# Two-layer hybrid diffusion block: ConvFFN down projections as seven block products, float32 activations kept on chip, six adaLN blocks moved earlier

## Chip, cores and metric

The kernel runs on one core of one Trainium2 chip. The metric is device time in microseconds of one execution; smaller is better. TensorE (PE in the rows) multiplies, VectorE (DVE) and ScalarE (ACT) prepare operands and empty the accumulator banks, and SyncE's queue (SP) issues every DMA of this kernel. PSUM has eight accumulator banks of 128x512 float32.

## What is computed

A latent stream of 1024 tokens and 1024 features passes two layers. Layer 0 mixes tokens by multi-scale pooling and windowed attention, layer 1 by a gated spatial MLP. Every layer ends with a ConvFFN, and every sublayer is normalized, modulated (adaLN: shift, scale, gate from a conditioning vector) and added to the stream:

```python
def post(x, y, g, gate):
    return x + gate * rmsnorm(y, g)

def conv_ffn(h, w_up, conv_w, conv_b, w_down):
    hu = h @ w_up                                   # 1024 -> 2*2816
    hcv = lax.conv_general_dilated(hu, conv_w[:, None, :], ...) + conv_b   # depthwise, width 3
    gate, up = jnp.split(hcv, 2, axis=-1)
    return (jax.nn.silu(gate) * up) @ w_down        # 2816 -> 1024: the down projection

    sh_m, sc_m, gt_m, sh_f, sc_f, gt_f = adaln(c, w_ada[i], b_ada[i])   # silu(c) @ w + b
    ...
    x = post(x, y, g_mix_post[i], gt_m)
    x = post(x, conv_ffn(pre(x, g_ffn_pre[i], sh_f, sc_f), ...), g_ffn_post[i], gt_f)
```

## The kernel before

**Precision.** Every large product takes its two float32 operands as a rounded part (float32r, "hi") and a remainder ("lo"). `three` (lines 123 to 127) issues three matmuls for each pair of tiles: hi by hi, hi by lo, lo by hi. Making the two parts of a 128x512 tile takes one copy on ScalarE and one subtraction on VectorE: `piece` (lines 113 to 121) does it for a weight tile that it loads into one of four `raw` buffers; its result goes into one of three `hl` buffers.

**Stages.** Layer 0: input projections (`u_proj`, `q_proj`), attention (16 units of `scores` and `attend`), output projection `e`, then `ffn`: the up projection with convolution and gating, which writes each of 22 gated feature blocks (128 features x 1024 tokens) to the DRAM tensor `act_d`, and the down projection `d`. Layer 1: projections `sv` and `su`, output projection `o`, `ffn` again. Instructions are written by hand in program order; a scheduler at build time turns this order into one fixed order for each engine and for SP's queue, and `tc.high_priority()` moves what stands under it ahead. Buffers are claimed when their former tile is done.

**Down projection before.** `load_acts(hf)` reads the 22 blocks of one token half (512 tokens), splits each into hi and lo and keeps them: eight blocks in the large rotating buffers `big` (six of 16 KB a partition), 14 in a pool of their own. `back_proj` then runs, for each output half `dh` and each of the 22 blocks, one `piece` of the weights and 12 matmuls into four banks (four blocks of 128 tokens). So one layer has 2 token halves x 2 output halves x 22 x 12 = 1056 matmuls. In layer 1 the second token half is done in two passes of two token blocks, so that each weight tile is split once more and serves six matmuls; the last of the post-processing then concerns two token blocks. Emptying a bank takes the sum of squares on ScalarE and a multiplication by the gate row `grows` on VectorE. `post_pair` (lines 272 to 306) normalizes two token blocks, adds the residual `xin` read from DRAM, stores the result, and, where a layer follows, normalizes again, transposes on TensorE and writes the modulated operand of the next stage.

**adaLN blocks.** `ada_sum(i)` reads a block of 1024x512 weights in four DMAs of 512 KB into the two `xtmp` buffers and does eight multiply-adds of 128x512 on VectorE into an `ntmp` buffer; `ada_finish(i)` sums over partitions on TensorE. Blocks 0 and 1 give a gate row and take two splits and two more DMAs. Blocks 0 and 1 stand at attention units 8 and 12, blocks 4, 5, 2, 3 behind the first half of the output projection `e`. The transposed probabilities `pt` of `attend` use the same two `xtmp` buffers.

Of the kernel before, what the change touches and what calls it, by code (L numbers as in the profile page):

```python
# [16 lines left out]
P = 128  # L17
# [24 lines left out]
def hybrid_block(ctx: ExitStack, tc: tile.TileContext, x, cx, cols_d, rows_d, cvw_d, rope_d, ident_d, mask_d, wada_a,  # L42
# [167 lines left out]
    def ada_sum(i):  # L210

        acc = ntmp(f"aacc{i}")[:, :HT]
        for q in range(4):
            raw = xtmp(f"ar{i}_{q}")
            nc.sync.dma_start(out=raw, in_=wada_b[i, q])
            for kk in range(2):
                k = 2 * q + kk
                w = raw[:, kk * HT:(kk + 1) * HT]
# [53 lines left out]
    def post_pair(y, hf, pair, ss, step, h, nxt, name, to_h=True):  # L272
# [23 lines left out]
        for kp in range(4):  # L296
            ps = bank(f"tr{name}{kp}")
            for kk in range(2):
                for i in range(2):
                    k = 2 * kp + kk  # L300
                    nc.tensor.transpose(out=ps[:, (2 * kk + i) * P:(2 * kk + i + 1) * P],
                                        in_=y[:, 2 * pair + i, k * P:(k + 1) * P], identity=ident)
            tsl = slice(2 * pair * P, 2 * (pair + 1) * P)
            modulated(ps, 2, 2 * P, 2 * kp, lambda k: gmod[:, l, w, k:k + 1],
                      lambda k: ada[:, l, 24 * w + k:24 * w + k + 1], h[0][:, 2 * kp:2 * kp + 2, tsl],
                      h[1][:, 2 * kp:2 * kp + 2, tsl], f"{name}{kp}", kp % 2 == 1)
# [13 lines left out]
    def post(ys, hf, step, nxt, name):  # L320
        h = hslots("h" + name) if nxt is not None else None
        for pair in range(2):
            post_pair(ys[0], hf, pair, ys[1], step, h, nxt, f"{name}{pair}")
# [45 lines left out]
    def ffn(l, pu, h0, tail, step, nxt, background=()):  # L369
# [163 lines left out]

        es = ExitStack()
        ap = es.enter_context(tc.tile_pool(name=f"act{l}", bufs=NF - 8, reuse_waits="tile"))
        act, acts_hh = {}, {}

        def new_act(f, hf):

            if f >= 8:  # L540
                return ap.tile([P, 2, HT], F32R, tag="a", name=f"a{l}_{f}_{hf}")
            s = f // 4
            if (s, hf) not in acts_hh:
                acts_hh[s, hf] = slot([P, 4, 2, HT], F32R, f"ah{l}_{s}_{hf}")
            return acts_hh[s, hf][:, f % 4]

        def load_acts(hf):
            for f in range(NF):
                raw = ntmp(f"arw{l}_{f}_{hf}")[:, :HT]
                nc.sync.dma_start(out=raw, in_=act_d[order[f]][:, halves(hf)])  # L550
                t = act[f] = new_act(f, hf)
                A.copy(out=t[:, 0, :], in_=raw)
                tt(t[:, 1, :], raw, t.bitcast(F32)[:, 0, :], ALU.subtract)

        def acts(f):
            return act[f][:, 0, :], act[f][:, 1, :]

        load_acts(0)
        ys = back_proj(pu, acts, lambda k: wdn[l, order[k]], NF, 0, step, f"d{l}")
        load_acts(1)  # L560
        h0 = post(ys, 0, step, nxt, f"f{l}0")
        if nxt is not None:
            ys = back_proj(pu, acts, lambda k: wdn[l, order[k]], NF, 1, step, f"d{l}")
            es.close()
            return h0, ys
        y = slot([P, 4, D], F32, f"yd{l}1")
        for pair in range(2):
            ys = back_proj(pu, acts, lambda k: wdn[l, order[k]], NF, 1, step, f"d{l}", (2 * pair, 2 * pair + 1), y)
            post_pair(y, 1, pair, ys[1], step, None, None, f"f{l}1{pair}")
# [3 lines left out]
    with ExitStack() as es:  # L573
# [123 lines left out]
        with tc.tile_pool(name="rope", bufs=1) as rp:  # L697
# [86 lines left out]
            for j in range(4):  # L784
                q_proj(j)

# [98 lines left out]
        order = [(n, kv) for n in range(8) for kv in range(2)]  # L885
        for i, (n, kv) in enumerate(order):
# [19 lines left out]
        for i in (4, 5, 2, 3):  # L906
            ada_block(i)
# [3 lines left out]
    h0, ys = ffn(0, pu, h0, lambda b22, ts: post_sums(ys, 0, (0, 1), "a1", h0, b22, ts), 1, (1, 0), range(6, 12))  # L911


    with ExitStack() as es:
        cs = es.enter_context(tc.tile_pool(name="cs", bufs=1))
# [41 lines left out]
        h.append(post(ys, 1, 1, (1, 0), "f01"))  # L957
# [5 lines left out]
        mp = es.enter_context(tc.tile_pool(name="mp", bufs=1))  # L963
# [129 lines left out]
```

## Time and profile before

| | us |
|---|---|
| three timed runs, median (lowest to highest) | 2151.49 (2147.37 to 2152.92) |
| the profiled execution, its own time | 2150.81 |
| its span, first to last instruction | 2149.0 |

The profile is of one execution, 1.8 us longer than its span. Busy time of an engine is the union of its instructions. Matmuls overlap in the pipeline, so that the rate is read from counts in a window and not from the duration of one.

### The profile page before, as it was taken

To read this page: it belongs to the slowest core of one execution; us is meant where nothing else is said; L and a number is where in the kernel's file an instruction comes from. 1 tells how busy PE (TensorE), PEld (TensorE's weight loads), DVE (VectorE), ACT (ScalarE), POOL (GpSimd) and SP (SyncE) were. 2 spreads that over 40 slices of the span, in tenths; PEclk is the share of its full clock that TensorE was granted. 3 is DMA by queue.
4 is the path that set the end of the run, shared out by engine and by line. 5 is a ranking of instruction groups with operands and counts; after the bars stand their busy time and mean duration, and the time that the engine had idled before them with its cause. 6 is when DMAs were issued, how large, how long until landed. Compare 5 with 4: busy or idle time off the path is not lost.

```text
span 2149.0 us, 26048 instructions
## 1 busy us (share of the span) xinstructions
PE 2083.5 (97%) x9334; PEld 1635.6 (76%) x9334; DVE 1523.3 (71%) x2403; ACT 1092.4 (51%) x1892; POOL 0.2 (0%) x4
## 2 busy tenths in 40 slices
PE   6999988999999999999999999999999999999998
PEld 2786545777877888888787888887878888888876
DVE  4687765668999987854634567467998897774655
ACT  5646754357555555544524432256655554553544
POOL 0000000000000000000000000000000000000000
PEclk8999999999999999999999999999999999999999
DMA  8110012747444442255524336346644222164675
GB/s 307 53 49 23 6 50 95 233 150 274 164 164 164 170 142 89 96 179 171 182 95 162 102 115 197 111 161 237 210 138 161 98 98 89 69 211 146 206 246 181
DMA packets 123985, 311.25 MB, mean 145 GB/s; under 512 B 13768, under 2 KB 14408, under 8 KB 123728
## 3 DMA queue, kind: packets, MB, share of 16 engines
q1 hardware_dynamic: 123856, 309.60, 43.1%
q8 instruction: 73, 1.20, 0.2%
q14 instruction: 56, 0.46, 0.1%
HBM read 260.26 MB, written 49.28 MB: 144 GB/s over the span
## 4 chain that ended last, share of the span: by engine, by line
PE 76%; DVE 10%; DMA 7%; ACT 4%; issue 2%; SPq 0%; DVEq 0%; ACTq 0%
PE d L126 6%; PE d L125 6%; PE d L127 6%; PE x L125 5%; PE x L127 4%; PE x L126 4%; PE o L869 3%; PE z L126 3%; PE z L125 3%; PE z L127 3%; DMA ar<-in_wada_b_dram 2%; DMA rawd<-in_wdn_dram 2%; PE xb L125 2%; PE xb L126 2%; PE xb L127 2%
## 5 line engine op out<-in xcount | busy, mean ns | idle before, releaser
L51 DVE TENSOR_TENSOR hld<-rawd,hld 128x512 fp32r<-128x512 f32 x220 | 150.8, 691 | 212.3 <-ACT hld L119 210.1
L119 ACT CAST hld<-rawd 128x512 fp32r<-128x512 f32 x220 | 136.7, 622 | 257.0 <-PE d L127 200.6
L398 ACT CAST w<-s 128x512 fp32r<-128x512 f32 x176 | 108.8, 620 | 226.1 <-PE z L127 107.5
L126 PE MATMUL d<-hld,a 128*128 128x512 f32 x448 | 175.1, 391 | 0.7 <-DVE hld L51 0.5
L125 PE MATMUL d<-hld,a 128*128 128x512 f32 x448 | 174.8, 390 | 0.2 <-ACT hld L119 0.2
L127 PE MATMUL d<-hld,a 128*128 128x512 f32 x448 | 174.4, 389 | 0.0
L51 DVE TENSOR_TENSOR w<-s,w 128x512 fp32r<-128x512 f32 x176 | 120.4, 686 | 32.9 <-ACT w L398 32.8
L48 DVE SCALAR_TENSOR_TENSOR aacc<-ar,silc,aacc 128x512 f32<-128x512 f32 x140 | 104.7, 748 | 20.7 <-DMA ar<-in_wada_b_dram 19.5
L48 DVE SCALAR_TENSOR_TENSOR au<-c,cvw,au 128x1023 f32<-128x1023 f32 x88 | 112.6, 1280 | 1.0
L126 PE MATMUL d<-hld,ah 128*128 128x512 f32 x256 | 100.2, 392 | 0.4 <-DVE hld L51 0.3
L127 PE MATMUL d<-hld,ah 128*128 128x512 f32 x256 | 99.7, 389 | 0.0
L125 PE MATMUL d<-hld,ah 128*128 128x512 f32 x256 | 99.6, 391 | 0.0
L126 PEld LDWEIGHTS d<-hld,a 128*128 128x128 f32 x448 | 84.1, 188 | 20.2 <-DVE hld L51 3.0
L125 PEld LDWEIGHTS d<-hld,a 128*128 128x128 f32 x448 | 84.1, 188 | 18.5 <-ACT hld L119 1.1
L127 PEld LDWEIGHTS d<-hld,a 128*128 128x128 f32 x448 | 84.1, 188 | 17.3
L869 PE MATMUL o<-pt,vv 128*64 128x512 f32 x152 | 78.7, 637 | 7.6 <-ACT pt L867 7.4
L125 PE MATMUL x<-t,w 128*128 128x512 f32 x208 | 82.0, 394 | 0.9 <-ACT c L477 0.9
L51 DVE TENSOR_TENSOR s<-raw 128x512 f32<-128x512 f32 x88 | 60.6, 689 | 29.7 <-DMA raw<-in_wup_dram 28.6
L126 PE MATMUL x<-t,w 128*128 128x512 f32 x208 | 81.4, 391 | 0.0
L127 PE MATMUL x<-t,w 128*128 128x512 f32 x208 | 81.3, 391 | 0.0
L127 PE MATMUL z<-b,w 128*128 128x512 f32 x176 | 69.3, 394 | 0.0
L126 PE MATMUL z<-b,w 128*128 128x512 f32 x176 | 69.3, 394 | 0.0
(458 smaller groups left out, 5596.5 us busy)
## 6 DMA issues: line engine op xcount, KB each, us to landing
rawd<-in_wdn_dram SPq DMA_DIRECT2D x220, 256.0 KB, 2.9
raw<-in_wup_dram SPq DMA_DIRECT2D x88, 512.0 KB, 4.5
ar<-in_wada_b_dram SPq DMA_DIRECT2D x80, 512.0 KB, 4.3
actd<-ag SPq DMA_DIRECT2D x44, 512.0 KB, 2.9
arw<-actd SPq DMA_DIRECT2D x88, 256.0 KB, 3.6
ra<-in_wup_dram SPq DMA_DIRECT2D x36, 256.0 KB, 3.4
leadd<-c SPq DMA_DIRECT2D x18, 512.0 KB, 4.2
aw<-in_wada_a_dram SPq DMA_DIRECT2D x16, 512.0 KB, 6.9
```

What stands on the lines that cost most here:

```text
L48: V.scalar_tensor_tensor(out=out, in0=in0, scalar=scalar, in1=in1, op0=op0, op1=op1)
L51: V.tensor_tensor(out=out, in0=in0, in1=in1, op=op)
L119: A.copy(out=hi, in_=raw)
L125: nc.tensor.matmul(ps, a[0], b[0], start=first, stop=False, skip_group_check=more)
L126: nc.tensor.matmul(ps, a[0], b[1], start=False, stop=False, skip_group_check=more)
L127: nc.tensor.matmul(ps, a[1], b[0], start=False, stop=last, skip_group_check=more)
L398: A.copy(out=t[:, 0, :], in_=src)
L869: nc.tensor.matmul(po, vv[:, kb, a], pt, start=c == 0, stop=c == nch - 1)
```

## The change

Both token halves are now in one product scheme. With the 22 feature blocks split in two halves j (11 each) and the output in two halves, each layer's down projection is a product of 2x2 blocks: A (token halves hf by feature halves j) times B (feature halves by output halves), done by seven block products of 11 steps with 12 matmuls each. The products run in the order 5, 1, 3, 6, 2, 7, 4, on two sets of four banks, and several accumulate onto a bank set that has been copied out. Their operands are sums and differences of blocks, formed on VectorE in float32 at each step and split into hi and lo at each step; two sums of weight blocks are written to DRAM scratch (`t1d`, `t2d`) and read again three products later. The activations stay as float32 in the six `big` buffers. Results collect in two tiles `ys` of a new pool; the gate row is now applied in `post_pair` (`gated=False`), with one more VectorE addition of 128x1024 for each token block and the modulation wholly on ScalarE. The second half of layer 1 is no longer done in pairs. adaLN blocks 0 and 1 go behind `q_proj(1)` and `q_proj(3)`; blocks 4, 5, 2, 3 go to attention units 3, 6, 9, 12, finish two units later, and load 256 KB at a time into the `raw` buffers.

```diff
-    def ada_sum(i):
+    def ada_sum(i, short=False):
+            if short:
+                ws = [raw_tile(f"as{i}_{q}{kk}") for kk in range(2)]
+                for kk in range(2):
+                    nc.sync.dma_start(out=ws[kk], in_=wada_b[i, q][:, halves(kk)])
...
-            stt(yb, yb, r[:, i:i + 1], xin, ALU.mult, ALU.add)
+            if gated:
+                stt(yb, yb, r[:, i:i + 1], xin, ALU.mult, ALU.add)
+            else:
+                stt(yb, yb, r[:, i:i + 1], grows[step], ALU.mult, ALU.mult)
+                tt(yb, yb, xin, ALU.add)
...
-        load_acts(0)
-        ys = back_proj(pu, acts, lambda k: wdn[l, order[k]], NF, 0, step, f"d{l}")
-        load_acts(1)
-        h0 = post(ys, 0, step, nxt, f"f{l}0")
...
+        dp = dn.enter_context(tc.tile_pool(name=f"dn{l}", bufs=3, reuse_waits="tile"))
...
+        def act(hf, j, k, load=False):
+            i = 2 * k + j
+            if (hf, i // 8) not in acts:
+                acts[hf, i // 8] = slot([P, 8, HT], F32, f"ac{l}_{hf}_{i // 8}")
+            t = acts[hf, i // 8][:, i % 8, :]
+            if load:
+                nc.sync.dma_start(out=t, in_=act_d[order[j * nh + k]][:, halves(hf)])
+            return t
...
+        def operands(prod, k):
+            if prod == 5:
+                s_ = act(1, 0, k, True)
+                tt(s_, s_, act(1, 1, k, True), ALU.add)
+                t_ = summed("t1" + nm, wload(0, k, 1, "b12" + nm), wload(0, k, 0, "b11" + nm), ALU.subtract, t1d, k)
+            elif prod == 1:
+                s_ = act(0, 0, k, True)
+                tt(act(1, 0, k), act(1, 0, k), s_, ALU.subtract)
+                t_ = wload(0, k, 0, "b11" + nm)
+            elif prod == 3:
+                s_ = summed("s4" + nm, act(0, 1, k, True), act(1, 0, k), ALU.subtract)
+                t_ = wload(1, k, 1, "b22" + nm)
+            elif prod == 6:
+                s_ = act(1, 0, k)
+                t_ = summed("t2" + nm, wload(1, k, 1, "b22" + nm), scratch(t1d, k, "t1r" + nm), ALU.subtract, t2d, k)
+            elif prod == 2:
+                s_ = act(0, 1, k)
+                t_ = wload(1, k, 0, "b21" + nm)
+            elif prod == 7:
+                s_ = summed("s3" + nm, act(1, 1, k), act(1, 0, k), ALU.subtract)
+                t_ = summed("t3" + nm, wload(1, k, 1, "b22" + nm), wload(0, k, 1, "b12" + nm), ALU.subtract)
+            else:
+                s_ = act(1, 1, k)
+                t_ = summed("t4" + nm, wload(1, k, 0, "b21" + nm), scratch(t2d, k, "t2r" + nm), ALU.subtract)
+            for src, pool, tag in ((s_, dp, "sa"), (t_, wp, "hl")):
+                t = pool.tile([P, 2, HT], F32R, tag=tag, name=f"{tag}{nm}")
+                A.copy(out=t[:, 0, :], in_=src)
+                tt(t[:, 1, :], src, t.bitcast(F32)[:, 0, :], ALU.subtract)
...
+        def down_product(prod, banks, first):
+            for k in range(nh):
+                with tc.high_priority():
+                    sa, w = operands(prod, k)
+                for b in range(4):
+                    three(banks[b], tuple(sa[:, i, b * P:(b + 1) * P] for i in range(2)), (w[:, 0, :], w[:, 1, :]),
+                          first and k == 0, k == nh - 1, not first)
...
+        y = y_banks("p5")
+        down_product(5, y, True)
+        evac(y, 1, 1, False, False)
+        x_ = [pu(f"px{l}{b}") for b in range(4)]
+        down_product(1, x_, True)
+        evac(x_, 0, 0, False, False)
+        down_product(3, y, False)
+        evac(y, 0, 1, False, False)
+        down_product(6, x_, False)
+        evac(x_, 0, 1, True, True)
+        y = y_banks("p2")
+        down_product(2, y, True)
+        evac(y, 0, 0, True, True)
+        h0 = post((ys[0], ss[0]), 0, step, nxt, f"f{l}0", False)
+        down_product(7, x_, False)
+        evac(x_, 1, 1, True, True)
+        down_product(4, x_, False)
+        evac(x_, 1, 0, False, True)
...
             for j in range(4):
                 q_proj(j)
+                if j in (1, 3):
+                    ada_block(j // 2)
...
+        late = {3: 4, 6: 5, 9: 2, 12: 3}
...
-            if i in (8, 12):
-                acc = ada_sum(i // 4 - 2)
-            if i in (9, 13):
-                ada_finish(i // 4 - 2, acc)
+            if i in late:
+                acc = ada_sum(late[i], True)
+            if i - 2 in late:
+                ada_finish(late[i - 2], acc)
...
-        for i in (4, 5, 2, 3):
-            ada_block(i)
```

## Rows read from the trace of the kernel before

**Rows 1.** The page: span, busy time by engine, the chain that ended last by engine.
```profile
span 2149.0 us, 26048 instructions
...
PE 2083.5 (97%) x9334; PEld 1635.6 (76%) x9334; DVE 1523.3 (71%) x2403; ACT 1092.4 (51%) x1892; POOL 0.2 (0%) x4
...
PE 76%; DVE 10%; DMA 7%; ACT 4%; issue 2%; SPq 0%; DVEq 0%; ACTq 0%
```

**Rows 2.** Windows: stretch, length; busy us (instructions) by engine, granted clock, DMA share, GB/s.
```profile
500.00:880.00 380.00, 376.67 (x1652) 304.11 (x1651) 344.09 (x469) 207.62 (x312) 0.00 (x0) 1.00 0.45 154
915.00:1161.00 246.00, 245.27 (x1093) 201.43 (x1092) 115.19 (x183) 100.59 (x187) 0.00 (x0) 1.00 0.46 149
1896.00:2140.00 244.00, 242.73 (x1057) 197.21 (x1056) 133.23 (x203) 112.99 (x202) 0.00 (x0) 1.00 0.63 200
...
1100.00:1150.00 50.00, 50.00 (x222) 41.19 (x221) 14.51 (x22) 12.66 (x25) 0.00 (x0) 1.00 0.31 97
```

**Rows 3.** The same view: stages of the adaLN blocks, in order q projections, attention, `e`.
```profile
110.00:160.00 50.00, 50.00 (x230) 41.36 (x228) 41.56 (x76) 23.76 (x41) 0.00 (x0) 1.00 0.16 50
...
270.00:290.00 20.00, 14.08 (x70) 7.71 (x69) 14.26 (x29) 9.33 (x21) 0.00 (x0) 0.91 0.37 129
...
320.00:350.00 30.00, 24.35 (x112) 13.56 (x112) 20.22 (x45) 15.09 (x33) 0.00 (x0) 0.83 0.27 88
380.00:400.00 20.00, 17.21 (x69) 13.66 (x69) 14.11 (x22) 6.16 (x14) 0.00 (x0) 0.91 0.67 223
```

**Rows 4.** Groups of instructions by form: line, engine, operation, count, busy us, mean ns.
```profile
L51 DVE TENSOR_TENSOR hld<-rawd,hld 128x512 fp32r<-128x512 f32 x220 | 150.8, 691 | 212.3 <-ACT hld L119 210.1 <-DMA arw<-actd 2.0
L119 ACT CAST hld<-rawd 128x512 fp32r<-128x512 f32 x220 | 136.7, 622 | 257.0 <-PE d L127 200.6 <-DMA rawd<-in_wdn_dram 24.3 <-DVE hld L51 19.7
...
L48 DVE SCALAR_TENSOR_TENSOR aacc<-ar,silc,aacc 128x512 f32<-128x512 f32 x140 | 104.7, 748 | 20.7 <-DMA ar<-in_wada_b_dram 19.5
```

**Rows 5.** Timeline of DVE near the end of layer 0's up projection: start, duration.
```profile
896.92 0.68 DVE L51 TENSOR_TENSOR ah<-arw,ah 128x512 fp32r<-128x512 f32 x1
897.51 0.68 DVE L51 TENSOR_TENSOR w<-s,w 128x512 fp32r<-128x512 f32 x1
898.12 1.28 DVE L51 TENSOR_TENSOR ah<-arw,ah 128x512 fp32r<-128x512 f32 x2
...
918.06 2.60 DVE L48 SCALAR_TENSOR_TENSOR au<-c,cvw,au 128x1023 f32<-128x1023 f32 x2
```

**Rows 6.** Windows of high and middling DMA load (columns as in rows 2).
```profile
10.00:20.00 10.00, 9.33 (x20) 1.76 (x18) 0.00 (x0) 3.31 (x6) 0.00 (x0) 1.00 1.02 414
...
2030.00:2070.00 40.00, 39.29 (x166) 30.42 (x165) 22.56 (x33) 18.14 (x33) 0.00 (x0) 1.00 0.81 270
2110.00:2140.00 30.00, 30.00 (x134) 24.86 (x133) 15.62 (x23) 13.82 (x25) 0.00 (x0) 1.00 0.53 158
```

**Rows 7.** DMA issues of 2030 to 2070: count, size, median us to landing.
```profile
rawd<-in_wdn_dram SPq DMA_DIRECT2D x29, 256.0 KB, 4.0
xinf<-x3d SPq DMA_DIRECT2D x4, 512.0 KB, 4.7
```

**Rows 8.** DMA issues of 2110 to 2140 (columns as in rows 7).
```profile
rawd<-in_wdn_dram SPq DMA_DIRECT2D x17, 256.0 KB, 3.0
```

**Rows 9.** Timeline of PE: end of the last first-stage product; bank change in `e`.
```profile
896.04 0.39 PE L125 MATMUL z<-b,w 128*128 128x512 f32 x1
...
392.06 0.50 PE L125 MATMUL e<-hle,hix 128*128 128x512 f32 x1 [2.79 <-DVE ye L51]
...
394.96 0.63 PE L125 MATMUL e<-hle,hix 128*128 128x512 f32 x1
```

**Rows 10.** Timeline of the last 10 us: ACT, DVE, SP.
```profile
2139.80 0.60 ACT L163 ACTIVATE junk<-d 128x512 bf16<-128x512 f32 x1 [2.78 <-PE d L127]
...
2142.97 2.48 DVE L48 SCALAR_TENSOR_TENSOR yd<-yd,rpf,xinf 128x1024 f32<-128x1024 f32 x2
...
2144.29 1.54 SPq L284 DMA_DIRECT2D out_dram<-yd  x2
```

More of the change, by code (lines that the diff above doesn't have):

```diff
@@ L208, in ada_first @@
             ALU.mult)
-    def ada_sum(i):
+    def ada_sum(i, short=False):
         acc = ntmp(f"aacc{i}")[:, :HT]
         for q in range(4):
-            raw = xtmp(f"ar{i}_{q}")
-            nc.sync.dma_start(out=raw, in_=wada_b[i, q])
+            if short:
[3 more added lines that the diff above has]
+            else:
+                raw = xtmp(f"ar{i}_{q}")
+                nc.sync.dma_start(out=raw, in_=wada_b[i, q])
+                ws = [raw[:, halves(kk)] for kk in range(2)]
             for kk in range(2):
                 k = 2 * q + kk
-                w = raw[:, kk * HT:(kk + 1) * HT]
+                w = ws[kk]
                 if k == 0:
@@ L269, in modulated, with post_pair @@
         tt(lo, fv, hi.bitcast(F32), ALU.subtract)
-    def post_pair(y, hf, pair, ss, step, h, nxt, name, to_h=True):
+    def post_pair(y, hf, pair, ss, step, h, nxt, name, to_h=True, gated=True):
         s2 = sm.tile([P, 2], F32, tag="s2", name="s2" + name)
@@ L318, in back_proj, with post @@
         return y, ss
-    def post(ys, hf, step, nxt, name):
+    def post(ys, hf, step, nxt, name, gated=True):
         h = hslots("h" + name) if nxt is not None else None
         for pair in range(2):
-            post_pair(ys[0], hf, pair, ys[1], step, h, nxt, f"{name}{pair}")
+            post_pair(ys[0], hf, pair, ys[1], step, h, nxt, f"{name}{pair}", gated=gated)
         return h
@@ L532, in ffn @@
             assert not background
+        nh = NF // 2
         es = ExitStack()
[L535 to L556, printed above, removed]
-        load_acts(0)
-        ys = back_proj(pu, acts, lambda k: wdn[l, order[k]], NF, 0, step, f"d{l}")
@@ L560, in ffn @@
-        load_acts(1)
-        h0 = post(ys, 0, step, nxt, f"f{l}0")
-        if nxt is not None:
[L563 to L569, printed above, removed]
+        yp = es.enter_context(tc.tile_pool(name=f"y{l}", bufs=2, side="right", reuse_waits="tile"))
@@ new lines, in wload, with scratch, summed @@
+        def wload(j, k, half, name):
+            t = raw_tile(name)
+            nc.sync.dma_start(out=t, in_=wdn[l, order[j * nh + k]][:, halves(half)])
+            return t
+        def scratch(t, k, name):
+            r = raw_tile(name)
+            nc.sync.dma_start(out=r, in_=t[k])
+            return r
+        def summed(name, in0, in1, op, keep=None, k=0):
+            t = dp.tile([P, HT], F32, tag="sum", name=name, bufs=4)
+            tt(t, in0, in1, op)
+            if keep is not None:
+                nc.sync.dma_start(out=keep[k], in_=t)
+            return t
@@ new lines, in down_product, with y_at, evac @@
+        def down_product(prod, banks, first):
[5 more added lines that the diff above has]
+                          first and k == 0, k == nh - 1, not first)
+        def y_at(hf, b, dh):
+            return ys[hf][:, b, halves(dh)]
+        def evac(banks, hf, dh, add, done):
+            for b in range(4):
+                if add:
+                    tt(y_at(hf, b, dh), banks[b], y_at(hf, b, dh), ALU.add)
+                else:
+                    A.copy(out=y_at(hf, b, dh), in_=banks[b])
+                if done:
+                    square_sum(y_at(hf, b, dh), ss[hf][:, 2 * b + dh:2 * b + dh + 1], HT)
@@ new lines, in y_banks @@
+        def y_banks(name):
+            return [mbank(f"{name}{l}0")] + [bank(f"{name}{l}{b}") for b in range(1, 4)]
+        y = y_banks("p5")
[9 more added lines that the diff above has]
+        y = y_banks("p2")
@@ L570, in ffn @@
+        down_product(2, y, True)
[5 more added lines that the diff above has]
+        evac(x_, 1, 0, False, True)
+        dn.close()
+        if nxt is not None:
+            return h0, (ys[1], ss[1]), es
+        post((ys[1], ss[1]), 1, step, None, f"f{l}1", False)
         es.close()
@@ L955, in v_norm @@
                                 scalar2=rs[:, n:n + 1], op0=ALU.subtract, op1=ALU.mult)
-        h.append(post(ys, 1, 1, (1, 0), "f01"))
+        h.append(post(ys, 1, 1, (1, 0), "f01", False))
+        ye.close()
         vs.append(slot([P, 4, D], F32, "vs1"))
@@ L962, in hybrid_block @@
         v_norm(1)
[L963 removed]
+        mp = es.enter_context(tc.tile_pool(name="mp", bufs=1, reuse_waits="tile"))
         ms = []
```

17 lines of the change are left out of this document (14 added, 3 removed).

## Prediction

> **What bounds the kernel now.** I read the page first: TensorE is busy 97% of the span and holds 76% of the chain that ended last; VectorE has 71% [rows 1]. Then the windows, stage by stage, since a mean hides limits. In the up projection TensorE is full and VectorE is at 344.09 of 380 us; in both down projections TensorE is full, VectorE has only 115 of 246 and 133 of 244 us [rows 2]. So the stage that is changed is bound by the number of its matmuls, with room on the engines that prepare operands. The rate is 222 matmuls in 50 us, 0.2252 us each, 2.70 us for a step of twelve, at a granted clock of 1.00, the 2.4 GHz level [rows 2]. Layer 1's stage holds 1057 in 244.0 us, where that rate would need 238.0: 6.0 us go to its passes over pairs, at their worst 166 matmuls in 40 us instead of 178 [rows 6]. The adaLN blocks have their own stages: TensorE idles 5.9 of 20 and 5.7 of 30 us around the two in attention, at clocks 0.91 and 0.83, and 2.8 of 20 us in `e` [rows 3].
>
> **What is removed.** Seven products of 11 steps of 12 are 924 matmuls a layer, 132 fewer than 1056. Two layers: 264 x 0.2252 = 59.5 us. The pairs of layer 1 go as well: 6.0 us. Together **-65.5**, if the new operands arrive in time. Four steps decide that.
>
> **VectorE and ScalarE in a step.** Before, a step needed one weight split and, half the time, one activation split. Now it needs two splits (two VectorE operations, two ScalarE copies) and sums: in the order 5, 1, 3, 6, 2, 7, 4 VectorE has 4, 3, 3, 3, 2, 4, 3 operations. ScalarE's two copies take 2 x 0.622 = 1.24 us of 2.70 [rows 4]: covered. One VectorE operation lasts 0.691 us [rows 4], which would make products 5 and 7 cost 2.76 us a step, more than TensorE. But queued ones start 0.59 and 0.61 us apart [rows 5], so four take 2.44. The Trainium skill ("VectorE: DVE Perf Modes", The DRAIN you can't avoid) has the next operation start only when the pipe is empty; starts closer than the duration disagree with it as I read it. By its rule the 44 steps of products 5 and 7 would cost 0.06 us more each, 2.6 us; by the rows nothing. I take the rows. The cover is thin: 0.26 us a step.
>
> **Start of product 5.** Layer 0's convolution still runs when the stage begins: VectorE does multiply-adds of 2.60 us a pair from 918.06 [rows 5], in all some 6 us behind 915, and its result is the last activation that product 5 loads. Slack in product 5 is 11 x 0.26 = 2.9 us. So 3 us late, per layer. The new operand pool also lies over buffers of the up projection, which come free with its last product: another 1 to 2 us (estimate: one chain of sum, copy and remainder, 0.61 + 0.62 + 0.69).
>
> **DMA.** Product 5 moves per step two activation tiles, two weight tiles and one scratch write, 5 x 262,144 bytes; 14.4 MB in 29.7 us. At 2030 to 2070 a share of 0.81 moved 270 GB/s, so a full share is 333, and 14.4 MB take 43 us [rows 6]. But the buffers of the up projection's first operand come free at 896.04 [rows 9], 19 us before 915, so 16 activation tiles (4.2 MB) can come early, and the remaining 10.2 MB need 31 us. Between 1 and 13 us late; with small transfers I take 4, as the rows of early release are direct. The Trainium skill ("DMA: Bandwidth & Descriptors", Specifications) gives about 358 GB/s as a core's HBM limit, which speaks against this product: 14.4 MB would take 40 us. The slice 10 to 20 moved 414 GB/s [rows 6], above that limit, so I do not use it; at 414 it would be 35. Start and DMA of product 5 together: 9 us a layer, **+18**, bounds +2 (all hidden) and +36 (18 a layer).
>
> Products 6, 7 and 4 also use two raw tiles a step, four buffers in all: two steps (5.40 us) must hold issue, landing, queueing and subtraction. Landing was 3.0 us at 158 GB/s and 4.0 at 270 [rows 6 to 8]. Product 6 runs at 3 x 262,144 / 2.70 us = 291 GB/s. Before, the same depth in time (four tiles of 1.35 us) lost 7% at 270 GB/s and nothing at 158 [rows 6]. So product 6 loses 7 to 8% of 29.7, 2.5 us a layer: **+5** (0 to 16). Products 7 and 4 need 194 GB/s, plus the residuals that `post` moves: 5%, or 1.5 us each, and between them the same four banks are reused at once, with VectorE adding each out; `e` lost 2.79 us at such a change, and matmuls of half clock (0.63 instead of 0.39) behind it [rows 9]. I take 1 here, since down stages show little such loss: **+8** for both layers (0 to 20).
>
> **post.** The gate row and the residual take two operations of about 1.22 us instead of one of 1.24 [rows 10]. For layer 0's first half VectorE has 4 x 2.44 + 8 x 0.61 + about 4 of normalizing = 19 us. Products 7 and 4 take 77 x 0.61 = 47, their bank adds and those before them 5: 71 us against 59.5 of matmuls and some 4 of transposes. Three buffers let 7.3 us be done earlier. The stage behind needs this result: **+3** (0 to 10). In layer 1 nobody waits for the first half; its rest falls into the end.
>
> **The end.** Now the last matmul ends at 2139.80 and the span at 2149.0: 9.2 us, with two multiply-adds, 2.48 us [rows 10]. Afterwards four token blocks are open, 4 x 2.44 = 9.8 us: 7.3 more, with two residual buffers whose loads take 4.7 us [rows 7], partly hidden. **+7** (5 to 10).
>
> **adaLN blocks.** A block is 8 multiply-adds, about 7 x 0.75 + 0.5 = 5.7 us of VectorE [rows 4]. In attention the two present blocks cost 5.9 + 5.7 us idle and up to 1.8 + 5.1 us of clock, 18 in all [rows 3]; there loads take `xtmp` buffers that the probabilities need. The four new ones use raw buffers, no gate row and smaller loads, but come four times: I leave 2 us each, gain 10 (bounds 0 and 18). `e` loses its four blocks: idle 2.8 and slow clock 1.8, gain 5 (0 to 8). The q projections get two blocks with gate splits, 15 us of VectorE where 8.4 of 50 are free and TensorE has no gap [rows 3]; later projections take the rest: cost 4 (0 to 10). Their DMAs are eight of 512 KB on SP's queue at a share of 0.16, hidden. Net **-11**.
>
> **Sum.** -65.5 - 11 + 18 + 5 + 8 + 3 + 7 = -35.5. The profiled execution took 2150.8, 0.7 below the median; 2150.8 - 35.5 = **2115 us**.
>
> **Rivals.**
> *Everything is covered.* TensorE full at the start of product 5 and through 6, 7, 4; only the end costs. 2150.8 - 65.5 - 11 + 7 + 2 = 2083. For it: VectorE's 242 operations a layer are 148 of 208 us. Against: 49 MB a layer in 208 us are 236 GB/s, over 149 and 200 before [rows 2].
> *VectorE paces products 5 and 7 and the posts.* If the 0.26 us of slack is lost to waits for ScalarE (0.62) in one of two steps, 44 x 0.31 = 14 us come on top, and 10 with the convolution's tail and `post`: 2115 + 24 = 2139. The up projection runs with VectorE at 91% and little loss [rows 2], which speaks against it.
> *Slower: the raw buffers' round trip.* In the 88 steps of products 5, 6, 7, 4 the time of a step is half a round trip: landing plus about 2.0 us (two issues, a place in VectorE's queue, 0.69). At landing 3.0 it is 2.5, hidden; at 4.0 it is 3.0, 26 us lost, near the 31 of my sum; at 5.5 it is 3.75: 92 us lost, 61 above the sum, 2176. It decides from 4.9 us of landing on (3.45 a step, 66 lost). 4.0 at 270 GB/s [rows 7] is short of that, but residuals took 4.7.
> *The change does little:* gains and new waits cancel, within 6.5 us (0.3%, about what a measurement here can tell): 2145 to 2158.
>
> **Chances.** Forecast (2095 to 2132) 0.55; all covered (2070 to 2095) 0.17; VectorE (2132 to 2145) 0.14; cancels 0.04; slower 0.10. That is faster 0.86, same 0.04, slower 0.10. The range leaves out most of the slower case and the best end: 2080 to 2150; the forecast's own is 2095 to 2132.
>
> **What would show it.** 1848 matmuls in the two down stages, each stage 215 to 235 us. Product 5 should show fewer than 222 in 50 us, products 1, 3 and 2 full. Landing of weight tiles near 4 us in 5 and 6. From the last matmul to the end 15 to 18 us. In attention no slice with 4 us of idle. Wrong: product 2 not full (then it is no operand problem), landing above 5, or VectorE above 95% through the stage.

## Result and profile after

The changed kernel takes 2165.15 us (median of four runs, 2160.87 to 2166.09) beside 2151.88 (2147.37 to 2152.92) for the kernel before on the same chip: ratio 1.0062 [1.0042, 1.0082], slower by 13 us. The forecast was 2115, range 2080 to 2150: wrong in sign. Its profiled execution took 2160.87 us.

The page of the changed kernel, the same lines as in [rows 1]:

```profile
span 2159.1 us, 25709 instructions
...
PE 2024.0 (94%) x9070; PEld 1586.3 (73%) x9070; DVE 1628.1 (75%) x2571; ACT 1109.4 (51%) x1940; POOL 0.2 (0%) x4
...
PE 68%; DVE 14%; DMA 11%; ACT 4%; issue 2%; SPq 1%; DVEq 0%; ACTq 0%
```

264 matmuls are gone, TensorE's busy time fell by 59.5 us, and the span grew by 10.1: on the chain, VectorE and DMA now hold 25% where they held 17%. The windows say in which stages. Up projection, layer 0's down stage, a middle product of it, layer 1's down stage (columns as in [rows 2]):

```profile
500.00:880.00 380.00, 377.26 (x1649) 305.75 (x1649) 340.97 (x458) 202.52 (x300) 0.00 (x0) 1.00 0.41 141
896.00:1153.00 257.00, 220.96 (x955) 179.07 (x956) 182.51 (x292) 125.02 (x236) 0.00 (x0) 0.92 0.58 193
960.00:1010.00 50.00, 50.00 (x222) 41.43 (x221) 28.57 (x45) 22.51 (x40) 0.00 (x0) 1.00 0.32 101
1889.00:2140.00 251.00, 215.29 (x924) 175.65 (x924) 172.83 (x271) 108.39 (x201) 0.00 (x0) 0.93 0.57 191
```

The count of matmuls is as forecast (924 a layer, 222 in 50 us where operands are there), but TensorE idles 36 us in each down stage. From the timelines, layer 0's down stage begins at 895.8 (915.4 before), lasts 257.5 us (245.2 before), layer 1's 251.1 (244.1), and the last matmul ends 19.4 us before the span does (8.7). So: 19.6 us won ahead of the first down stage, 12.3 and 7.0 lost in the two, 10.7 lost at the end.

TensorE's longest waits, changed kernel (total, times, longest):

```profile
PE p L125 <- ACT hld L614: 30.1, 2, 15.6
PE p L126 <- DVE hld L51: 20.8, 2, 10.8
PE px L125 <- DVE yd L51: 19.4, 3, 9.6
```

`p` is product 5, `px` here product 4. Four waits at the start of product 5 (two a layer) and one a layer at the change from product 7 to 4 are 70 us. Layer 0's first wait in the timeline of PE, then of SP:

```profile
911.36 2.07 PE L125 MATMUL p<-hld,sad 128*128 128x512 f32 x4 [15.56 <-ACT hld L614]
923.44 0.79 PE L126 MATMUL p<-hld,sad 128*128 128x512 f32 x1 [10.01 <-DVE hld L51]
```

```profile
875.13 0.33 SPq L571 DMA_DIRECT2D b12d<-in_wdn_dram  x1
876.25 27.96 SPq L566 DMA_DIRECT2D ac<-actd  x40
904.58 0.33 SPq L571 DMA_DIRECT2D b11d<-in_wdn_dram  x1
905.26 0.33 SPq L571 DMA_DIRECT2D b12d<-in_wdn_dram  x1
```

Step 0 needs b12 and b11. The first is issued at 875, the second at 904.6: between them SP issues 40 of the 44 activation loads, both token halves, product 3's too. They had free buffers and the operands' priority; the weights, four raw buffers, did not. This is what the early release did that the prediction counted as a gain (16 tiles ahead of time).

### The profile page after: what moved, and what is told of

Read it like the earlier page. It is cut to its first block, busy times and chain, and to the rows that moved or that the text cites. A ratio compares the mean times of both kernels' runs of the same rounds, so it can differ in the third digit from the quotient of the medians.

```text
span 2159.1 us, 25709 instructions
## 1 busy us (share of the span) xinstructions
PE 2024.0 (94%) x9070; PEld 1586.3 (73%) x9070; DVE 1628.1 (75%) x2571; ACT 1109.4 (51%) x1940; POOL 0.2 (0%) x4
## 4 chain that ended last, share of the span: by engine, by line
PE 68%; DVE 14%; DMA 11%; ACT 4%; issue 2%; SPq 1%; DVEq 0%; ACTq 0%
PE x L125 4%; PE x L127 4%; PE x L126 4%; PE o L965 3%; PE z L126 3%; PE z L125 3%; PE z L127 3%; PE p L126 2%; PE px L126 2%; PE px L125 2%; PE p L127 2%; PE px L127 2%; DMA ac<-actd 2%; PE p L125 2%; DMA t1rd<-t1d 2%
## 5 line engine op out<-in xcount | busy, mean ns | idle before, releaser
L125 PE MATMUL px<-hld,sad 128*128 128x512 f32 x352 | 139.1, 396 | 19.4 <-DVE yd L51 19.4
L614 ACT CAST sad<-ac 128x512 fp32r<-128x512 f32 x110 | 68.2, 622 | 165.2 <-PE px L127 80.0
L126 PE MATMUL px<-hld,sad 128*128 128x512 f32 x352 | 139.4, 396 | 1.8 <-DVE hld L51 1.8
L127 PE MATMUL px<-hld,sad 128*128 128x512 f32 x352 | 138.1, 393 | 0.0
L125 PE MATMUL p<-hld,sad 128*128 128x512 f32 x264 | 104.4, 400 | 30.1 <-ACT hld L614 30.1
L126 PE MATMUL p<-hld,sad 128*128 128x512 f32 x264 | 105.5, 400 | 20.8 <-DVE hld L51 20.8
L51 DVE TENSOR_TENSOR sad<-ac,sad 128x512 fp32r<-128x512 f32 x110 | 75.7, 689 | 55.8 <-ACT sad L614 55.6
L127 PE MATMUL p<-hld,sad 128*128 128x512 f32 x264 | 105.1, 398 | 0.0
L125 PEld LDWEIGHTS px<-hld,sad 128*128 128x128 f32 x352 | 67.0, 190 | 35.0 <-issue 19.9
L48 DVE SCALAR_TENSOR_TENSOR aacc<-ar,silc,aacc 128x512 f32<-128x512 f32 x112 | 83.9, 749 | 10.8 <-DMA ar<-in_wada_b_dram 9.4
L125 PEld LDWEIGHTS p<-hld,sad 128*128 128x128 f32 x264 | 50.9, 194 | 41.6 <-ACT hld L614 31.0
L126 PEld LDWEIGHTS px<-hld,sad 128*128 128x128 f32 x352 | 66.9, 190 | 18.5 <-DVE hld L51 5.1
L127 PEld LDWEIGHTS px<-hld,sad 128*128 128x128 f32 x352 | 66.7, 190 | 13.6
L126 PEld LDWEIGHTS p<-hld,sad 128*128 128x128 f32 x264 | 50.9, 193 | 32.9 <-DVE hld L51 22.3
```

Of the source, the lines that this page charges most:

```text
L48: V.scalar_tensor_tensor(out=out, in0=in0, scalar=scalar, in1=in1, op0=op0, op1=op1)
L51: V.tensor_tensor(out=out, in0=in0, in1=in1, op=op)
L125: nc.tensor.matmul(ps, a[0], b[0], start=first, stop=False, skip_group_check=more)
L126: nc.tensor.matmul(ps, a[0], b[1], start=False, stop=False, skip_group_check=more)
L127: nc.tensor.matmul(ps, a[1], b[0], start=False, stop=last, skip_group_check=more)
L614: A.copy(out=t[:, 0, :], in_=src)
```

## Experiments

Comparisons are with the changed kernel's 2165.2 and, as ratios, with the kernel before, which took 2149.4 to 2150.3 beside these runs and 2151.9 beside the changed kernel. So a difference from 2165.2 is uncertain by some 2 us; where that matters, the difference by the ratios is given too.

**1. The adaLN move alone**, on the kernel before: blocks 0 and 1 behind the q projections 1 and 3, blocks 4, 5, 2, 3 into attention with short loads.

```diff
+                if j in (1, 3):
+                    ada_block(j // 2)
...
+            if i in late:
+                acc = ada_sum(late[i], True)
...
-        for i in (4, 5, 2, 3):
-            ada_block(i)
```

> The kernel before with the adaLN blocks of layer 0 moved and nothing else (down projections as before). The prediction had 11 us of gain for this part. The trace of the changed kernel enters its first down projection at 895.8 instead of 915.4 us. If these 19.6 us belong to the move, the time falls by 18 to 21 us; if part of them comes from another order that the new down projection leads to, by 8 to 15 us.

Measured 2130.3 us, ratio 0.9913 [0.9893, 0.9932]: 20 us won, the 19.6 that the changed kernel gains ahead of its first down stage. In it and in the changed kernel alike, two windows of [rows 3] are now (this run; attention, then `e`):

```profile
320.00:350.00 30.00, 29.02 (x142) 15.53 (x143) 17.94 (x45) 19.52 (x45) 0.00 (x0) 1.00 0.00 1
380.00:400.00 20.00, 20.00 (x89) 16.33 (x89) 7.43 (x11) 7.21 (x16) 0.00 (x0) 1.00 0.31 99
```

The first of them holds no adaLN load any more (a DMA share of 0.00; the four blocks' multiply-adds now stand between 207 and 282), so it says nothing of their cost. The stages do. The first matmul of `e` and the first one behind `e`, in the kernel before and in this run:

```profile
360.31 0.48 PE L125 MATMUL e<-hle,hix 128*128 128x512 f32 x1
...
475.38 0.39 PE L125 MATMUL x<-hiha,wa 128*128 128x512 f32 x1
```

```profile
357.01 0.48 PE L125 MATMUL e<-hle,hix 128*128 128x512 f32 x1
...
455.86 0.39 PE L125 MATMUL x<-hiha,wa 128*128 128x512 f32 x1
```

`e` takes 98.9 us in place of 115.1, 16.2 less. Attention's first matmul of scores comes 3.3 us later than before (149.2 and 145.9), and attention takes 207.8 us in place of 214.4.

So the change of the down projections itself costs about 35 us against the kernel with the move alone (2165.2 - 2130.3).

**2. Queue order.** Each activation load is placed behind the weight load of the step that needs it some steps later.

```diff
+                behind = wl.get((5, k - 3) if hf == 1 else (5, min(5 + k, nh - 1)) if j == 0 else (1, k))
+                with tc.issue_after(behind.ins) if behind is not None else nullcontext():
+                    nc.sync.dma_start(out=t, in_=act_d[order[j * nh + k]][:, halves(hf)])
```

> The changed kernel with the same loads in another order on SP's queue: an activation load of product 5 stands behind the weight loads three steps before it, the 22 loads of the other token half behind weight loads of products 5 and 1. No byte less. In the changed kernel product 5 takes 59.7 us in layer 0 (895.8 to 955.5) where its 132 matmuls need 29.7. Queue theory (SP sends 40 activation loads, 28 us of its time, before the second weight tile of step 0): the two waits of 15.6 and 10.0 us go, product 5 takes 32 to 37 us in each layer, and the time falls by 45 to 55 us to 2110 to 2120. Volume theory (product 5 needs more bytes than can be moved in its time): the 22 later loads (5.8 MB) leave it, 14.4 MB at about 340 GB/s stay, product 5 takes 42 us or more and the time falls by 35 us or less.

2156.7 us, ratio 1.0024 [1.0014, 1.0035]: 8.5 us, not 45. The first wait fell from 15.6 to 7.7 and others came in its place; product 5 of layer 0 still took 53 us. VectorE's timeline of this run shows what step 0 now waits for:

```profile
895.82 2.60 DVE L48 SCALAR_TENSOR_TENSOR au<-c,cvw,au 128x1023 f32<-128x1023 f32 x2
898.52 1.23 DVE L51 TENSOR_TENSOR ag<-ag,au 128x1024 f32<-128x1024 f32 x1
899.66 1.29 DVE L51 TENSOR_TENSOR t1d<-b12d,b11d 128x512 f32<-128x512 f32 x2
```

Both weight tiles were issued by 875.3, and their sum is taken at 899.66, without any idle time in front: it stands in VectorE's order behind the whole convolution of the last block.

**3. Activation loads from GpSimd's queue** in place of SP's.

```diff
-                nc.sync.dma_start(out=t, in_=act_d[order[j * nh + k]][:, halves(hf)])
+                nc.gpsimd.dma_start(out=t, in_=act_d[order[j * nh + k]][:, halves(hf)])
```

> The changed kernel with the activation loads of both token halves issued from GpSimd's queue instead of SP's: the same loads, as early as buffers allow, but no weight load and no write of an activation block stands behind them on a queue. Queue theory: the first weight tiles leave SP at once and share the DMA engines with the loads; product 5 loses 5 to 15 us instead of 30 in each layer, the time falls by 25 to 50 us. Volume theory: the bytes before the first steps are the same, product 5 still loses 20 us or more, the time falls by less than 20 us.

2165.5 us, ratio 1.0077 [1.0053, 1.0101]: nothing. Freeing SP shortened the first wait to 7.2 us, as in experiment 2, and a wait of 11.4 for a split activation followed. A freed queue alone is not enough.

**4. Is it the address?** By the order of allocation the new pool's first sum tile should lie at the address of the convolution's weights. A gap of 704 bytes moves it, on top of experiment 2.

```diff
+        gap = dp.tile([P, 176], F32, tag="gap", name=f"gap{l}", bufs=1)
```

> The activation loads issued in the order of need, and besides a gap of 704 bytes at the head of the new operand pool, so that the first sum tile doesn't lie over the convolution's weights. Address theory: the first wait of product 5 falls from 7.7 us to 2 or 3 in each layer, 2157 - 10 = 2147 us. Queue theory (the sums are late because SP's weight loads of step 2 stand behind the writes of blocks 20 and 21): the first step comes earlier, but the wait only moves to step 2; 2155 us or more.

2156.9 us, ratio 1.0031 [1.0016, 1.0045]; first waits 7.2 and 7.7. The address theory falls.

**5. All remedies seen so far at once**: queue order, gap, activations written from GpSimd's queue (in experiment 2 SP stood 8.7 us at the last two writes), product 1's subtraction behind product 5's sums, the adds between 7 and 4 first.

```diff
-                nc.sync.dma_start(out=act_d[f], in_=g)
+                nc.gpsimd.dma_start(out=act_d[f], in_=g)
...
+                with tc.issue_after(wl["t"].ins):
+                    tt(act(1, 0, k), act(1, 0, k), s_, ALU.subtract)
...
+        with tc.high_priority():
+            evac(x_, 1, 1, True, True)
```

> All that was seen at product 5's start at once: loads in the order of need, the gap, the writes of the activations from GpSimd's queue, product 1's subtraction behind product 5's last sum on VectorE; and the adds between products 7 and 4 first. Dependency theory: product 5 takes 35 to 40 us in place of 59.7, the bank waits fall to 4; 2160 - 2 x 21 - 8 = about 2112 us. Volume theory (product 5's 14.4 MB can't arrive in its 30 us in any order): product 5 stays above 47 us, 2135 us or more.

2160.5 us, ratio 1.0037 [1.0019, 1.0055], a clear miss: first waits 7.7 and 7.7 as in experiment 2. The waits at the change of banks fell to 2 or 2.5 us, and a wait of 4.5 appeared behind layer 0. Neither SP's stand at the writes nor the order of product 1's subtraction held the first step back.

**6. Outside the new pool.** Every tile of the pool `dn`, opened after `up` is closed, was dealt with behind the convolution, wherever it lay; tiles of older pools (`hld`, `ac`) were not. So, on top of experiment 2, the split activations and sums of product 5's first four steps go to `xtmp` and `ntmp`, which exist all along.

```diff
+            if keep is t1d and k < 4:
+                t = ntmp(name)[:, :HT]
...
+                if prod == 5 and k < 4 and tag == "sa":
+                    t = xp.tile([P, D], F32R, tag="x", name=f"{tag}{nm}").rearrange("p (i t) -> p i t", i=2)
...
+                    if prod == 5:
+                        for i in lastsplit:
+                            behind.enter_context(tc.issue_after(i.ins))
```

> The order of products as in the change, the activation loads in the order of need, and for the first four steps of product 5 the split activations and the sums in buffers that existed all along (the two of 4 KB that post uses, and the four small ones) in place of the new pool; all of product 5's operand work behind the up projection's last split on VectorE and ScalarE. Pool theory (a tile of the new pool comes, in the engines' instruction order, behind everything that used the old pool, the last convolution too, wherever it lies, which is why the gap of 704 bytes did nothing): the first wait of product 5 falls from 7.5 us to under 2 in both layers; the other waits (about 8 in layer 0, by the flow of bytes) stay: 2157 - 12 to 16 = 2141 to 2145 us. Volume theory: the waits move to the next steps, the stage is no shorter: 2153 or more.

2140.9 us, ratio 0.9958 [0.9942, 0.9974]: 15.8 us less than experiment 2, as the pool theory said, and faster than before. VectorE's timeline of this run:

```profile
885.77 0.68 DVE L51 TENSOR_TENSOR wd<-raw,wd 128x512 fp32r<-128x512 f32 x1
...
889.38 1.29 DVE L51 TENSOR_TENSOR t1d<-b12d,b11d 128x512 f32<-128x512 f32 x2
...
896.80 0.68 DVE L51 TENSOR_TENSOR c<-z,c 128x512 f32<-128x512 f32 x1
```

The sums are now taken at 889.38, ahead of the last convolution, and product 5 starts at 891.60 without a wait. It still takes 48.9 us to its last matmul, of which 2.8 belong to twelve matmuls of the up projection that now stand inside it (895.68 to 898.48). Its longest wait in layer 0 is 4.3 us, and the windows show what that one costs:

```profile
906.00:911.50 5.50, 1.19 (x6) 0.65 (x4) 5.40 (x8) 2.49 (x6) 0.00 (x0) 0.98 0.89 353
911.50:916.00 4.50, 3.78 (x8) 2.58 (x9) 2.91 (x5) 0.61 (x1) 0.00 (x0) 0.50 0.99 322
916.00:920.00 4.00, 4.00 (x14) 3.20 (x14) 2.50 (x4) 1.24 (x2) 0.00 (x0) 0.74 1.01 363
920.00:925.00 5.00, 5.00 (x23) 4.13 (x22) 4.25 (x8) 1.77 (x3) 0.00 (x0) 1.00 1.05 390
```

TensorE stood for 4.3 us; then the granted clock is 0.50, the 1.2 GHz level, and 22 matmuls take 8.5 us where 0.2252 us each would be 5.0.

The DMA share is 0.89 to 1.05 in these windows, but the wait isn't one for bytes. It is the wait for step 4, the first step whose split activation and sum lie in the new pool again (rows of SP, VectorE and PE):

```profile
894.63 0.56 SPq L577 DMA_DIRECT2D b11d<-in_wdn_dram  x1
...
908.97 1.23 DVE L51 TENSOR_TENSOR ag<-ag,au 128x1024 f32<-128x1024 f32 x1
910.11 1.29 DVE L51 TENSOR_TENSOR t1d<-b12d,b11d 128x512 f32<-128x512 f32 x2
...
911.50 1.65 PE L125 MATMUL p<-hld,sad 128*128 128x512 f32 x3 [4.31 <-ACT hld L626]
```

Step 4's second weight tile was issued at 894.63, and no weight tile of product 5 took longer than 7.2 us to land. Its sum is taken at 910.11, right behind the convolution's last operation, as step 0's was in experiment 2. Layer 1 shows the same (1890.97, then 1892.12; a wait of 4.28). The last lines of the edit (product 5's operands behind the up projection's last split) hold for all eleven steps alike, so what parts steps 0 to 3 from step 4 is the pool. What those lines would do alone was not run.

**7. The pool alone**, with the queue order of the change.

> The changed kernel with its queue order as it is (40 of 44 activation loads ahead of step 0's second weight tile), and only the first four steps' split activations and sums of product 5 in buffers that existed all along. If the pool alone held the first step back: about 2165 - 15 = 2150 us. If queue order and pool are in series (step 0's second weight tile still lands at 909 or later, whatever buffer the sum goes to): the first wait stays at 13 to 16 us, 2162 us or more.

2155.0 us, ratio 1.0031 [1.0015, 1.0047], between the two theories: the first wait stays at 16.6 us in layer 0, as the series theory said, while the second falls from 10.0 to 1.7 and 1.2, which neither foresaw. Order alone gave 8.5 us, pool alone 10.2, both 24.3 (by the ratios 8, 7 and 22): the two delays are partly in series.

**8. Bytes.** Experiment 6 without the 22 writes of product 5's sums; product 6 reads a weight tile in place of the sum, so that the result is another.

```diff
-                t_ = summed("t1" + nm, ..., ALU.subtract, t1d, k)
+                t_ = summed("t1" + nm, ..., ALU.subtract, k=k)
...
-                ... scratch(t1d, k, "t1r" + nm) ...
+                ... wload(0, k, 1, "t1r" + nm) ...
```

> The version with loads in the order of need and the first four steps outside the new pool (2140.9 us), without the 22 writes of product 5's sum to DRAM; product 6 reads a weight tile in place of that sum, so the result isn't the reference's, and product 6's loads stay as many. It takes 2.9 of 14.4 MB out of each product 5. Volume theory for what is left there (4.3 + 2.7 + 1.4 us of waits and half clock behind them, a DMA share of 0.95 to 0.96 at 331 to 343 GB/s): 2.9 MB at 340 GB/s are 8.5 us, so these waits go: 2141 - 12 to 17 = 2124 to 2129 us. If the waits come from VectorE's four operations a step, nothing changes: 2138 or more.

2128.9 us, ratio 0.9913 [0.9889, 0.9937]: 12 us less (10 by the ratios), at the volume theory's end. With 2.9 MB less, product 5 of layer 0 takes 44.3 us in place of 48.9, of layer 1 42.3 in place of 49.1, each with 2.8 us of the up projection inside. But the theory had counted three waits, and the one of 4.3 us is still there: 4.2 us in each layer, with half clock behind it, again for step 4's sum (taken at 920.42 in layer 0, behind the convolution's operation of 919.28). That is the pool, not the bytes; what went are the smaller waits. The edit takes 22 issues of some 0.6 us off SP's queue together with the bytes, and no run separates the two. What else is left over 29.7 stays open.

**9. The change of banks.** The adds that empty the banks of product 7 go ahead of product 4's operands on VectorE. In the changed kernel they stood behind them:

```profile
1116.68 0.68 DVE L51 TENSOR_TENSOR yd<-px,yd 128x512 f32<-128x512 f32 x1
1117.28 1.21 DVE L51 TENSOR_TENSOR yd<-yd,xinf 128x1024 f32<-128x1024 f32 x1
1118.41 1.88 DVE L51 TENSOR_TENSOR yd<-px,yd 128x512 f32<-128x512 f32 x3
```

The last matmul of product 7 ended at 1108; 1103 to 1115 went to operands of product 4 up to step 6 and to `post`.

```diff
+        with tc.high_priority():
+            evac(x_, 1, 1, True, True)
```

> The changed kernel with the additions that empty the four banks of product 7 moved ahead on VectorE, before operands of later steps of product 4 and before the post-processing of the first token half. In the changed kernel TensorE waits 9.5 and 9.6 us there. Order theory (the additions stand behind work that is not urgent): the wait falls to 3 us or less in each layer, with the slow clock behind it, and the time falls by 14 to 22 us. Theory of a full VectorE (products 7 and 4 with the post-processing need more of VectorE than there is): the additions come earlier but operands later, TensorE waits elsewhere in product 4, and the time falls by less than 6 us.

2160.2 us, ratio 1.0048 [1.0031, 1.0065]: waits at the change 19.1 to 3.9 us, gain only 5, and 3 by the ratios, whose intervals overlap with the changed kernel's. Layer 0's part is lost again in the next stage: products 7 and 4 take 66.3 us in place of 75.4, but `sv` behind them takes 107.4 in place of 96.5, with new waits of 4.5 us for `vs` and 1.1 for a transpose. That stage needs `post`, whose work on VectorE the changed kernel does in part while TensorE waits for the banks (1107.9 to 1118.4).

**10. Product 1 first**: order 1, 5, 3, 6, 2, 7, 4, so that product 5's loads have another 30 us. Loads stand in the order of need, and the gap is in.

```diff
+        x_ = [pu(f"px{l}{b}") for b in range(4)]
+        down_product(1, x_, True)
+        evac(x_, 0, 0, False, False)
         y = y_banks("p5")
         down_product(5, y, True)
         evac(y, 1, 1, False, False)
```

> The order of products alone: 1, 5, 3, 6, 2, 7, 4 (product 1 needs one activation tile and one weight tile a step and no sum; its subtraction moves into product 3's step), loads in the order of need, with the gap. Volume theory: product 1 gives the loads of product 5 another 30 us, so that products 1 and 5 together take 60 to 65 us where they took 90 (layer 0): 2160 - 2 x 26 = about 2108 us. Dependency theory without volume: the convolution's tail and the writes of blocks 20 and 21 now stand under product 1, which doesn't need them: the same, 2108. If product 5 is slow by itself (four VectorE operations, two ScalarE copies, a scratch write a step), it still takes 40 us or more in the second place: 2130 or more.

2154.4 us, ratio 1.0022 [1.0007, 1.0036]; expected 2108. Product 5 is nearly full in the second place (158 matmuls from 940 to 980, of 178; 33.6 us in layer 0), so most of its time in the first place isn't its own. But product 1 waits at its start, in its place (the first row is the change of banks, the others are the start):

```profile
PE px L125 <- DVE yd L51: 9.8, 1, 9.8
PE px L127 <- DVE sad L51: 8.4, 1, 8.4
PE px L125 <- ACT sad L619: 4.0, 1, 4.0
```

It needs two loads a step and still loses 12 us: its split activation is in the new pool, and two of product 5's in-place sums, which waited 1.7 us for a load, stand in front of it on VectorE too. With this run the volume alone is out as the cause of the first waits; experiment 6 was made after it.

**11. Product 1 first with the other remedies**: the adds of experiment 9, writes from GpSimd, and the gate row multiplied in as the last product of a column half leaves its banks, so that one multiply-add per block is left at the end.

```diff
+                    tt(y_at(hf, b, dh), y_at(hf, b, dh) if add else banks[b], grows[step][:, halves(dh)], ALU.mult)
...
-        post((ys[1], ss[1]), 1, step, None, f"f{l}1", False)
+        post((ys[1], ss[1]), 1, step, None, f"f{l}1")
```

> As the run with product 1 first, with the adds between products 7 and 4 ahead of product 4's operands, the activations written from GpSimd's queue, and the gate row multiplied in as the last product of a column half is taken out of its banks, so that at the end one multiply-add per token block is left. Against that run: bank waits from 19 to 4 us, of which layer 0's part may go to the stage behind (gain 8 to 15); the end from 19.4 to 14 us. 2085 to 2097 us if that run is near 2108.

2135.7 us, ratio 0.9921 [0.9894, 0.9948]: 18.7 less than experiment 10, the size expected, from a worse start.

**12. The same with product 1's first four split activations outside the new pool** and product 5's in-place sums behind product 1's splits.

```diff
+                if prod == 1 and k < 4 and tag == "sa":
+                    t = xp.tile([P, D], F32R, tag="x", name=f"{tag}{nm}").rearrange("p (i t) -> p i t", i=2)
...
+                with tc.issue_after(wl["v", 1, min(k + 2, nh - 1)].ins):
+                    tt(s_, s_, r_, ALU.add)
```

> The best version so far (product 1 first, loads in the order of need, adds between products 7 and 4 ahead, gate row multiplied in early; 2135.7 us) with three more edits at the stage's start: product 1's first four split activations in the two 4 KB buffers that existed all along, product 5's in-place sums behind product 1's splits on VectorE, the first seven activation loads behind nothing. Pool theory: the two waits at the start (4.0 and 8.1 us in layer 0, 4.0 and 8.4 in layer 1) and about 3 us of half clock behind each go: 2135.7 - 24 to 30 = 2106 to 2112 us. If the start is bound by the arrival of bytes, 2130 or more.

2115.0 us (2113.4 to 2116.2), ratio 0.9835 [0.9806, 0.9864], faster than before by 34 us and than the adaLN move alone by 15. The start (windows of this run; before this edit 63 and 43 matmuls, clock 0.91 and 0.67):

```profile
880.00:900.00 20.00, 19.98 (x87) 15.95 (x87) 14.92 (x17) 13.26 (x19) 0.53 (x1) 1.00 0.96 328
900.00:920.00 20.00, 16.95 (x65) 12.57 (x64) 15.23 (x23) 6.66 (x12) 0.53 (x1) 0.91 0.88 320
```

20.7 us were won where 24 to 30 were expected: three waits of 0.8 to 1.2 us with a stretch at 0.66 behind them remain, the longest again at step 4. So the seven products with all of this gain 15 us over the adaLN move alone.

## Why the prediction was wrong

**What is removed (-65.5): right.** 1848 matmuls; 222 in 50 us in products 1, 3 and 2.

**adaLN blocks (-11): right mechanism, one term mis-sized.** -19.6 by the first down stage, -20 alone. In the changed kernel the q projections cost 3.8 us (4 forecast) and attention gains 7.1 (10 forecast), but `e` gains 16.2 where the forecast had 5 (experiment 1 has nearly the same three numbers). That 5 came from one window, 380 to 400; `e` lasted from 360 to 475 and had a longer wait outside it, 4.2 us at 449 in the kernel before.

**Start of product 5 and DMA (+18, bounds +2 and +36): the step that failed.** Product 5 took 59.8 us in layer 0 (895.8 to 955.6) and 58.3 in layer 1 in place of 29.7: +58.6. Three statements in it were wrong. First, "16 activation tiles (4.2 MB) can come early": 40 came, and they stood ahead of the second weight tile of step 0. I had looked at when buffers come free, and not at what SP, which issues in order, would put into the free time. Second, the new pool "over buffers of the up projection" was to cost "another 1 to 2 us"; its tiles were handled behind the whole last convolution: with the order of loads changed and the first four steps' tiles outside the pool, 24.3 us came back (experiments 2, 6, 7), and a wait of 4.3 us with half clock behind it moved to step 4; the gap (experiment 4) shows that it isn't the shared address. Third, the flow: 4 us a layer were taken from a bound of 1 to 13; taking away a fifth of the bytes, and their issues, gives 5 to 6 us a layer (experiment 8), more than the 4 taken; how much all the bytes cost is not shown. The Trainium skill ("DMA: Bandwidth & Descriptors", Specifications) gives about 358 GB/s as a core's HBM limit, half of a stack's 716. This kernel runs on one core, and in the changed kernel 905 to 911 moved 396 GB/s, so the trace disagrees with that as a bound here, as slice 10 to 20 did [rows 6]:

```profile
905.00:911.00 6.00, 0.00 (x0) 0.00 (x0) 4.71 (x7) 1.45 (x3) 0.00 (x0) 0.50 1.05 396
```

No term for product 5 held the clock: each wait of 4 us in this stage has matmuls at 1.2 GHz behind it, about 3 us more (experiment 6).

**Product 6 (+5): right.** It takes 32.7 us in layer 0 and 31.3 in layer 1 in place of 29.9 (a full product in this trace), 4.2 in all, and VectorE stands up to 1.5 us a step for the load of `t1d`, the round trip that the prediction had named.

**Products 7 and 4 (+8): mis-sized in one term.** The change of banks was counted at 1 us, "since down stages show little such loss". It took 9.5 and 9.6 us, with nine matmuls in the 4 us behind it at clocks 0.54 and 0.55: about 23 in all. The row of `e` with its 2.79 us [rows 9] was the nearest, and too small too: there VectorE had little else in its queue, here product 4's operands for six steps.

**post (+3): no wait of its own** until the banks are emptied early (experiment 9): then the stage behind layer 0 takes 10.9 us longer. It had been covered by the wait for the banks, so moving the adds won nothing in layer 0.

**The end (+7): +10.7.** (The prediction took the last matmul's end from ScalarE's first operation, 2139.80; TensorE's last matmul starts at 2140.06.) Before the multiply-adds four copies and four sums of squares of the same banks pass ScalarE (2137.8 to 2142.6), and the last residual comes late:

```profile
2148.43 2.48 DVE L48 SCALAR_TENSOR_TENSOR yd<-yd,rpf,grow 128x1024 f32<-128x1024 f32 x2
2152.91 2.51 DVE L51 TENSOR_TENSOR yd<-yd,xinf 128x1024 f32<-128x1024 f32 x2 [2.00 <-DMA xinf<-x3d]
```

Its load can only be issued when one of the two buffers is free, at 2147.86. In experiment 12, with half of the arithmetic, the end still takes 16.0 us, 4.7 of them waiting for this load.

**The sum with measured terms**: -65.5 - 19.6 + 58.6 + 4.2 + 23 + 10.7 = +11.4, where the span grew by 10.1.

**The rivals.** The one that ended slower (2176) named the raw buffers' round trip, deciding from a landing of 4.9 us on. The weight tiles of product 5 landed in 4.2 us (median, layer 0; 4.3 and 4.8 in layer 1), and TensorE was full between 933 and 955; so the rival came near the time by another mechanism, and is not confirmed. VectorE as the pace of 5 and 7 fell too: in layer 0 of the changed kernel product 7 takes 29.9 us, a full product, and in that stretch of product 5 VectorE has 19.46 of 22 us while TensorE is full:

```profile
933.00:955.00 22.00, 22.00 (x98) 18.21 (x97) 19.46 (x32) 10.04 (x19) 0.00 (x0) 1.00 0.62 199
```

## What to carry to other kernels

When an edit frees buffers earlier, write down what the issuing queue will put into the freed time, in its order, and ask whether it is what the next step needs first: a prefetch without a limit can starve the first step. In these runs the tiles of a pool opened over a closed one were dealt with behind the old pool's last user; keep the first steps' tiles in buffers that live across the border, and as many steps as the old pool's last work lasts: four were too few here. Starting a stage with the step that needs the fewest bytes and sums may help too; experiment 10 alone gained nothing clear, and only together with the other remedies was it fast. Read what an edit is worth from whole stages: a window at a fixed time can hold other work afterwards. Count the emptying of banks by what is queued in front of it on the engine that empties them, and a wait of a few microseconds together with the half clock behind it.

## What the hardware showed besides

- After 4.3 us without a matmul in a stage otherwise full, the granted clock went from 0.98 to 0.50 and the next 22 matmuls took 3.5 us more, 0.7 of them a further wait; TensorE was back at 1.00 in the third window (experiment 6).
- A full DMA share (0.99 to 1.05) moved between 322 and 396 GB/s in these kernels (experiment 6; 905 to 911 of the changed kernel), depending on the stretch; my 333, worked out from a share of 0.81, was one value in this spread.
- Issuing the activation loads from another queue shortened the first wait from 15.6 to 7.2 us and left the time where it was (2165.5 us, experiment 3): the wait came back at a later step.
